# Closing a ReLU-and-mean kernel with one VectorE instruction over the last piece and the sums of the others

## The chip, the cores and the metric

The kernel runs on one core of one Trainium2 chip. The metric is the time of one execution on the device in microseconds, as the median of several runs. The engines that matter are DVE (VectorE), ACT (ScalarE), POOL (GpSimd), and SP (SyncE), which issues the transfers.

## The reference

```python
def reference(x):                       # x: float32, 32 x 512 x 1024
    relu_x = np.maximum(x, 0)
    return np.mean(relu_x, axis=-1).astype(np.float32)
```

There are 16384 rows of 1024 values, 67.11 MB in all; each row gives one number.

## The kernel before

Each of the 128 partitions holds 128 rows. Tiles of 16 rows are loaded through three buffers. ACT takes the even rows and DVE the odd rows; either makes ReLU and row sum in one instruction with an accumulator, whose read is a separate entry in the trace (0.08 us on DVE, 0.19 us on ACT). The last tile is loaded in ever smaller transfers, and its last row in three pieces of 512, 256 and 256 columns, so that little is left to do when the last bytes land. The end of the kernel is what the change is about:

```python
def act_row(nc, src, acc):
    nc.scalar.activation(out=src, in_=src, func=ACT.Relu, accum_out=acc)

def dve_row(nc, src, acc, init=None):
    nc.vector.tensor_scalar(out=src, in0=src, scalar1=0.0, scalar2=init,
                            op0=ALU.max, op1=ALU.add, accum_out=acc)
# ... loads and sums of all rows but the last two of each partition ...
    act_row(nc, prev[:, :512], part[:, 0:1])          # second-to-last row
    dve_row(nc, prev[:, 512:], part[:, 1:2])
    nc.gpsimd.tensor_scalar(out=res[:, J-2:J-1], ...)  # (a + b) * inv
    act_row(nc, last[:, :256], part[:, 2:3])          # piece 1, both engines
    dve_row(nc, last[:, 256:512], part[:, 3:4])
    nc.gpsimd.tensor_scalar(out=part[:, 4:5], ...)     # ACT's sum * inv
    act_row(nc, last[:, 512:640], part[:, 5:6])       # piece 2, both engines
    dve_row(nc, last[:, 640:768], part[:, 6:7], init=part[:, 3:4])
    nc.scalar.activation(out=part[:, 7:8], ...)        # ACT's two sums, scaled
    dve_row(nc, last[:, 768:], part[:, 8:9], init=part[:, 6:7])   # piece 3
    nc.vector.scalar_tensor_tensor(                    # closing: one column
        out=res[:, J-1:J], in0=part[:, 8:9], scalar=inv, in1=part[:, 7:8],
        op0=ALU.mult, op1=ALU.add)
    nc.sync.dma_start(out=outr, in_=res)
```

Of the kernel before, what the change touches and what calls it, by code (L numbers as in the profile page):

```python
# [1 line left out]

# [4 lines left out]

F32 = mybir.dt.float32
ALU = mybir.AluOpType
ACT = mybir.ActivationFunctionType  # L10
# [9 lines that stand above are left out]
    nc.vector.tensor_scalar(  # L20
        out=src, in0=src, scalar1=0.0, scalar2=init,
        op0=ALU.max, op1=ALU.add, accum_out=acc,
    )


def issue_ahead_of_entry_barrier(nc):


    entry, body = nc.cur_f.blocks[0].instructions, None
    for block in nc.cur_f.blocks[1:]:  # L30
        for k, ins in enumerate(block.instructions):
            if ins.opcode == "DMACopy":
                body, load = block.instructions, k
                break
        if body is not None:
            break
    first = body[load]
    assert first.engine == mybir.EngineType.SP and not first.sync_info.on_wait
    assert all(i.opcode == "DMACopy" or i.engine != first.engine for i in body[:load])
    del body[load]  # L40
    at = next(k for k, i in enumerate(entry) if i.engine == first.engine and i.opcode == "Drain")
    entry.insert(at, first)


@with_exitstack
def kernel(
    ctx: ExitStack,
    tc: tile.TileContext,
    x: bass.AP,
    out: bass.AP,  # L50
):
    nc = tc.nc
    P = nc.NUM_PARTITIONS
    xf = x.flatten_outer_dims()
    R, D = xf.shape
    assert R % P == 0
    J = R // P
    inv = 1.0 / D
    xr = xf.rearrange("(p j) d -> p j d", p=P, j=J)
    outr = out.flatten().rearrange("(p j) -> p j", p=P, j=J)  # L60
    xlast = xr[:, J - 1, :]

    NB = 16
    full = J // NB - 1

    row_pieces = [8, 4, 2, 1]
    assert sum(row_pieces) == NB - 1
    col_pieces = [512, 256, 256]
    assert sum(col_pieces) == D

    pools = ctx.enter_context(ExitStack())
    in_pool = pools.enter_context(tc.tile_pool(name="in", bufs=3))
    res_pool = pools.enter_context(tc.tile_pool(name="res", bufs=1))
    sums = res_pool.tile([P, J], F32)
    res = res_pool.tile([P, J], F32)
    part = res_pool.tile([P, 10], F32)

    def rows(xt, lo, n, j0):

        for k in range(lo, lo + n):  # L80
            j = j0 + k
            (dve_row if j % 2 else act_row)(nc, xt[:, k, :], sums[:, j:j + 1])

    def finish(lo, hi):
        nc.gpsimd.tensor_scalar(  # L85
            out=res[:, lo:hi], in0=sums[:, lo:hi], scalar1=inv, scalar2=0.0, op0=ALU.mult, op1=ALU.add,
        )

    for t in range(full):
        j0 = t * NB  # L90
        xt = in_pool.tile([P, NB, D], F32, name="xt")
        nc.sync.dma_start(out=xt, in_=xr[:, j0:j0 + NB, :])  # L92
        rows(xt, 0, NB, j0)

    j0 = full * NB
    xt = in_pool.tile([P, NB, D], F32, name="xt")
    prev, last = xt[:, NB - 2, :], xt[:, NB - 1, :]
    lo = 0
    for n in row_pieces:
        nc.sync.dma_start(out=xt[:, lo:lo + n, :], in_=xr[:, j0 + lo:j0 + lo + n, :])  # L100
        lo += n
    c = 0
    for w in col_pieces:
        nc.sync.dma_start(out=last[:, c:c + w], in_=xlast[:, c:c + w])
        c += w

    finish(0, j0)
    lo = 0
    for n in row_pieces[:-1]:
        rows(xt, lo, n, j0)  # L110
        lo += n
    finish(j0, j0 + lo)



    act_row(nc, prev[:, :512], part[:, 0:1])
    dve_row(nc, prev[:, 512:], part[:, 1:2])
    nc.gpsimd.tensor_scalar(  # L118
        out=res[:, J - 2:J - 1], in0=part[:, 0:1], scalar1=part[:, 1:2], scalar2=inv, op0=ALU.add, op1=ALU.mult,
    )  # L120
    act_row(nc, last[:, :256], part[:, 2:3])
    dve_row(nc, last[:, 256:512], part[:, 3:4])
    nc.gpsimd.tensor_scalar(  # L123
        out=part[:, 4:5], in0=part[:, 2:3], scalar1=inv, scalar2=0.0, op0=ALU.mult, op1=ALU.add,
    )
    act_row(nc, last[:, 512:640], part[:, 5:6])
    dve_row(nc, last[:, 640:768], part[:, 6:7], init=part[:, 3:4])
    nc.scalar.activation(  # L128
        out=part[:, 7:8], in_=part[:, 5:6], func=ACT.Identity, scale=inv, bias=part[:, 4:5],
    )  # L130
    dve_row(nc, last[:, 768:], part[:, 8:9], init=part[:, 6:7])
    nc.vector.scalar_tensor_tensor(  # L132
        out=res[:, J - 1:J], in0=part[:, 8:9], scalar=inv, in1=part[:, 7:8], op0=ALU.mult, op1=ALU.add,
    )
    nc.sync.dma_start(out=outr, in_=res)

    pools.close()
    tc.close()
    tc.compile()
    issue_ahead_of_entry_barrier(nc)  # L140


# [1 line left out]
_INS = ['x']  # L144
_OUTS = [((32, 512), 'float32')]


# [23 lines left out]
```

## Time and profile before

| | before |
|---|---|
| median time (3 runs) | 164.05 us (163.62 to 164.06) |
| profiled run: time, span | 163.88 us, 162.1 us |
| DVE, ACT, POOL busy | 46%, 43%, 1% |
| input transfer on the chain that ended last | 84% |

The chain that ended last is followed back from the last instruction. It says that the kernel is a long transfer with a short computation at its end. I use two marks throughout. **T0** is the start of the second-to-last row's first instruction (157.34 us before); what comes ahead of it is transfer. The **tail** runs from T0 to the end of the instruction that makes the last result (159.59), 2.25 us. The lines behind both are in the prediction below.

### The profile page before, as it was taken

The numbers are of one execution on the slowest core, as the hardware profiler recorded it, in microseconds if no ns is written. First come the engines' busy times: TensorE is split into PE (matmuls) and PEld (weight loads), VectorE is DVE, ScalarE is ACT, GpSimd is POOL, SyncE is SP. The second block draws the span as 40 slices with busy tenths as digits, with TensorE's granted clock in tenths as the row PEclk, the third lists the DMA queues.
The fourth block names the chain that finished last, engine by engine and source line by source line (L and its number), as shares of the span: only waits on it lengthen the run. The fifth ranks groups of instructions, "written<-read, shape, count | busy, mean of one in ns | idle before, by whom it ended". The sixth has DMA issues, their size and how long they took to land.

```text
span 162.1 us, 358 instructions
## 1 busy us (share of the span) xinstructions
DVE 74.7 (46%) x135; ACT 69.6 (43%) x134; POOL 1.2 (1%) x8
## 2 busy tenths in 40 slices
DVE  0000049700795009930199102990049800698993
ACT  3000049500793009910199002980049600696882
POOL 0000000000000000000000000000000000000001
DMA  8996996997997998998998999899898897998980
GB/s 275 501 485 291 518 501 291 501 501 323 469 518 340 437 518 356 420 518 356 420 520 374 404 501 404 388 501 404 388 518 388 388 518 332 437 445 384 420 311 17
DMA packets 2162, 67.19 MB, mean 415 GB/s; under 512 B 240, under 2 KB 624, under 8 KB 880
## 3 DMA queue, kind: packets, MB, share of 16 engines
q1 hardware_dynamic: 2160, 67.18, 96.6%
q14 instruction: 2, 0.02, 0.0%
HBM read 67.11 MB, written 0.07 MB: 414 GB/s over the span
## 4 chain that ended last, share of the span: by engine, by line
DMA 84%; DVE 13%; SPq 1%; issue 0%; DVEq 0%
DMA xt<-in_x_dram 84%; DVE xt L20 13%; SPq L100 1%; DVE res L132 0%; DVEq L20 0%; DVEq L132 0%; SPq L92 0%
## 5 line engine op out<-in xcount | busy, mean ns | idle before, releaser
L20 DVE TENSOR_SCALAR_CACHE_REDUCE xt<-xt 128x1024 f32<-128x1024 f32 (+1 forms) x65 | 73.7, 1195 | 84.7 <-DMA xt<-in_x_dram 84.3
L15 ACT ACTIVATE xt<-xt 128x1024 f32<-128x1024 f32 (+1 forms) x66 | 67.0, 1015 | 88.7 <-DMA xt<-in_x_dram 88.6
L15 ACT ACTIVATION_READ_ACCUMULATOR xt<-xt 128x1 f32 x66 | 12.3, 186 | 0.0
L20 DVE DVE_READ_ACCUMULATOR xt<-xt 128x1 f32 x65 | 5.4, 83 | 0.0
L85 POOL TENSOR_SCALAR res<-sums 128x112 f32<-128x112 f32 (+1 forms) x2 | 0.5, 252 | 156.7 <-DVE xt L20 156.7
L15 ACT ACT_TABLE_LOAD x1 | 1.3, 1283 | 0.8 <-PEq L155 0.8
L20 DVE TENSOR_SCALAR_CACHE_REDUCE xt<-xt,part 128x128 f32<-128x128 f32 (+1 forms) x2 | 0.8, 412 | 0.1
L128 ACT ACTIVATE part<-part 128x1 f32<-128x1 f32 x1 | 0.3, 294 | 0.1
L118 POOL TENSOR_SCALAR res<-part 128x1 f32<-128x1 f32 x1 | 0.3, 264 | 0.5 <-ACT xt L15 0.5
L132 DVE SCALAR_TENSOR_TENSOR res<-part 128x1 f32<-128x1 f32 x1 | 0.2, 159 | 0.1
L123 POOL TENSOR_SCALAR part<-part 128x1 f32<-128x1 f32 x1 | 0.2, 191 | 0.1
L20 DVE DVE_READ_ACCUMULATOR xt<-xt,part 128x1 f32 x2 | 0.2, 83 | 0.0
L155 POOL MEMSET const-bfloat16-1.0<- 128x1 bf16 x1 | 0.1, 101 | 0.0
L155 POOL MEMSET const-uint8-127<- 128x1 uint8 x1 | 0.1, 101 | 0.0
L155 POOL MEMSET const-float32-0.0<- 128x1 f32 x1 | 0.1, 98 | 0.2 <-issue 0.2
L155 POOL MEMSET const-float32-1.0<- 128x1 f32 x1 | 0.1, 98 | 0.0
## 6 DMA issues: line engine op xcount, KB each, us to landing
xt<-in_x_dram SPq DMA_DIRECT2D x1, 4096.0 KB, 39.0
xt<-in_x_dram SPq DMA_DIRECT2D x1, 2048.0 KB, 43.5
xt<-in_x_dram SPq DMA_DIRECT2D x1, 1024.0 KB, 45.5
xt<-in_x_dram SPq DMA_DIRECT2D x1, 512.0 KB, 46.4
xt<-in_x_dram SPq DMA_DIRECT2D x1, 256.0 KB, 46.5
xt<-in_x_dram SPq DMA_DIRECT2D x2, 128.0 KB, 42.7
xt<-in_x_dram SPq DMA_DIRECT2D x7, 49.1
out_dram<-res SPq DMA_DIRECT2D x1, 64.0 KB, 1.5
```

What stands on the lines that cost most here:

```text
L15: nc.scalar.activation(out=src, in_=src, func=ACT.Relu, accum_out=acc)
L20: nc.vector.tensor_scalar(out=src, in0=src, scalar1=0.0, scalar2=init, op0=ALU.max, op1=ALU.add, accum_out=acc,)
L85: nc.gpsimd.tensor_scalar(out=res[:, lo:hi], in0=sums[:, lo:hi], scalar1=inv, scalar2=0.0, op0=ALU.mult, op1=ALU.add,)
L100: nc.sync.dma_start(out=xt[:, lo:lo + n, :], in_=xr[:, j0 + lo:j0 + lo + n, :])
L118: nc.gpsimd.tensor_scalar(out=res[:, J - 2:J - 1], in0=part[:, 0:1], scalar1=part[:, 1:2], scalar2=inv, op0=ALU.add, op1=ALU.mult,)
L123: nc.gpsimd.tensor_scalar(out=part[:, 4:5], in0=part[:, 2:3], scalar1=inv, scalar2=0.0, op0=ALU.mult, op1=ALU.add,)
L128: nc.scalar.activation(out=part[:, 7:8], in_=part[:, 5:6], func=ACT.Identity, scale=inv, bias=part[:, 4:5],)
L132: nc.vector.scalar_tensor_tensor(out=res[:, J - 1:J], in0=part[:, 8:9], scalar=inv, in1=part[:, 7:8], op0=ALU.mult, op1=ALU.add,)
L155: nc = _bacc.Bacc("TRN2", target_bir_lowering=False, num_devices=1)
```

## The change

The last row gets a tile of its own, with two further columns. ACT takes the whole of piece 1 and DVE the whole of piece 2, and their sums go into these two columns, right behind piece 3. One scalar-tensor-tensor over the 258 columns then takes the maximum with 0 (which leaves the two sums as they are), multiplies by a tile filled with 1/1024, and accumulates: its accumulator is the mean. The intent is to get rid of the chain of small instructions that combines partial sums, above all of the last one.

```diff
-    part = res_pool.tile([P, 10], F32)
+    part = res_pool.tile([P, 2], F32)
+    last = res_pool.tile([P, D + 2], F32)
+    scale = res_pool.tile([P, D // 4 + 2], F32)
+    nc.gpsimd.memset(scale, inv)
...
-    act_row(nc, prev[:, :512], part[:, 0:1])
-    dve_row(nc, prev[:, 512:], part[:, 1:2])
+    act_row(nc, prev[:, :448], part[:, 0:1])
+    dve_row(nc, prev[:, 448:], part[:, 1:2])
...
-    (pieces 1 and 2 on both engines, the POOL and ACT scalings, piece 3)
+    act_row(nc, last[:, :512], last[:, D:D + 1])
+    dve_row(nc, last[:, 512:768], last[:, D + 1:D + 2])
     nc.vector.scalar_tensor_tensor(
-        out=res[:, J - 1:J], in0=part[:, 8:9], scalar=inv, in1=part[:, 7:8], op0=ALU.mult, op1=ALU.add,
+        out=last[:, 768:], in0=last[:, 768:], scalar=0.0, in1=scale, op0=ALU.max, op1=ALU.mult,
+        accum_out=res[:, J - 1:J],
     )
```

More of the change, by code (lines that the diff above doesn't have):

```diff
@@ L96 @@
     xt = in_pool.tile([P, NB, D], F32, name="xt")
-    prev, last = xt[:, NB - 2, :], xt[:, NB - 1, :]
+    prev = xt[:, NB - 2, :]
     lo = 0
@@ L120 @@
     )
-    act_row(nc, last[:, :256], part[:, 2:3])
-    dve_row(nc, last[:, 256:512], part[:, 3:4])
-    nc.gpsimd.tensor_scalar(
-        out=part[:, 4:5], in0=part[:, 2:3], scalar1=inv, scalar2=0.0, op0=ALU.mult, op1=ALU.add,
-    )
-    act_row(nc, last[:, 512:640], part[:, 5:6])
-    dve_row(nc, last[:, 640:768], part[:, 6:7], init=part[:, 3:4])
-    nc.scalar.activation(
-        out=part[:, 7:8], in_=part[:, 5:6], func=ACT.Identity, scale=inv, bias=part[:, 4:5],
-    )
-    dve_row(nc, last[:, 768:], part[:, 8:9], init=part[:, 6:7])
+    act_row(nc, last[:, :512], last[:, D:D + 1])
+    dve_row(nc, last[:, 512:768], last[:, D + 1:D + 2])
     nc.vector.scalar_tensor_tensor(
-        out=res[:, J - 1:J], in0=part[:, 8:9], scalar=inv, in1=part[:, 7:8], op0=ALU.mult, op1=ALU.add,
+        out=last[:, 768:], in0=last[:, 768:], scalar=0.0, in1=scale, op0=ALU.max, op1=ALU.mult,
+        accum_out=res[:, J - 1:J],
     )
```

## The prediction

> **What bounds the kernel now.** I read the page's busy row and its chain first, to see which resource carries the span:
>
> ```profile
> DVE 74.7 (46%) x135; ACT 69.6 (43%) x134; POOL 1.2 (1%) x8
> ...
> DMA 84%; DVE 13%; SPq 1%; issue 0%; DVEq 0%
> ...
> HBM read 67.11 MB, written 0.07 MB: 414 GB/s over the span
> ```
>
> Neither compute engine is half busy, and 84% of the chain is input transfer; 67.11 MB must come in, and the change takes no byte away. Only what follows the last bytes can move. So I read next when the last pieces land. The views of DMA issues, asked for one narrow stretch at a time, give for the three pieces of the last row (512, 256 and 256 columns) the issue and the time to landing; the timeline of the queue gives the start of each issue.
>
> ```profile
> 111.44 0.44 SPq L104 DMA_DIRECT2D xt<-in_x_dram  x1
> ...
> xt<-in_x_dram SPq DMA_DIRECT2D x1, 256.0 KB, 46.5
> ...
> xt<-in_x_dram SPq DMA_DIRECT2D x1, 128.0 KB, 46.4
> ...
> 119.59 0.33 SPq L104 DMA_DIRECT2D xt<-in_x_dram  x1
> ...
> xt<-in_x_dram SPq DMA_DIRECT2D x1, 128.0 KB, 39.0
> ```
>
> Piece 1 lands at 111.44 + 46.5 = 157.94. Piece 2's issue follows at about 111.93 (two issues end at 112.37, each 0.44 long), so it lands at 158.33. Piece 3 lands at 119.59 + 39.0 = 158.59. These are good to about 0.05 us, since the landing times are rounded. The second-to-last row lands at 157.31, where the chain changes from transfer to DVE. Then the timeline of the tail, from which the chain's DVE steps can be read off:
>
> ```profile
> 157.34 0.69 DVE L20 TENSOR_SCALAR_CACHE_REDUCE xt<-xt 128x512 f32<-128x512 f32 x1
> ...
> 157.97 0.42 DVE L20 TENSOR_SCALAR_CACHE_REDUCE xt<-xt 128x256 f32<-128x256 f32 x1
> ...
> 158.44 0.35 DVE L20 TENSOR_SCALAR_CACHE_REDUCE xt<-xt,part 128x128 f32<-128x128 f32 x1
> ...
> 158.83 0.48 DVE L20 TENSOR_SCALAR_CACHE_REDUCE xt<-xt,part 128x256 f32<-128x256 f32 x1
> 158.87 0.29 ACT L128 ACTIVATE part<-part 128x1 f32<-128x1 f32 x1
> 159.23 0.08 DVE L20 DVE_READ_ACCUMULATOR xt<-xt,part 128x1 f32 x1
> 159.43 0.16 DVE L132 SCALAR_TENSOR_TENSOR res<-part 128x1 f32<-128x1 f32 x1
> 159.65 0.35 SPq L135 DMA_DIRECT2D out_dram<-res  x1
> ```
>
> (The reader's columns are start, length, engine, line, operation.) The reader is to see that the row's last value is ready at 159.43 + 0.16 = 159.59, one microsecond after the last piece landed, and that all of the change lies in the 2.2 us between 157.34 and there. 2.2 us is 1.4% of the span, so even a tail of no length at all would not be a change of 2%.
>
> [...] the issues last 0.33 to 0.44 us, the landings are 39 to 46.5 us away, so I go by landings. [...] 1215, 685 and 419 ns for 1024, 512 and 256 columns are 1.04 ns a column plus 0.15 us. [...] The trace of before has this operation only on one column (159 ns), which can't decide it.
>
> **The change part by part.**
>
> *Removed:* on ACT the 128-column piece and the one-column scaling (0.29 + 0.29), on POOL the scaling of a partial sum (0.19), on DVE the 128-column reduction (0.35 + 0.08) and the closing one-column operation. On the path to the end the last costs 0.16 us plus the 0.12 us between the accumulator read's end (159.31) and its start[...]: 0.28 us that really go. ACT's and POOL's removed work ended at 159.16, beside DVE's, so it is worth nothing of its own.
>
> *Moved:* the second-to-last row is split 448/576 in place of 512/512. ACT's part becomes 0.05 us shorter (0.83 ns a column from its 630 and 416 ns), DVE's 64 x 1.04 = 0.07 us longer. DVE is then free at 157.97 + 0.07 = 158.04, and next needs piece 2 (158.33); ACT is free at 157.92 and next needs piece 1 (157.94). Both wait for landings anyway: worth 0.
>
> *Piece 1* goes wholly to ACT. Start 157.97; the 512-column activation before took from 157.34 to the end of its accumulator read at 157.87 + 0.19 = 158.06, that is 0.72 us. So its sum is there at 158.69[...].
>
> *Piece 2* goes wholly to DVE: start 158.33 + 0.03 = 158.36; 256 columns with accumulator read took 157.97 to 158.40 = 0.43 us, so the sum is there at 158.79.
>
> *The closing instruction* waits for DVE's own sum, ACT's sum, piece 3 (158.59) and the fill of the scale tile (over since the start). In the built program these four are spread over two event waits ahead of it and one on it, with DVE's own sum first. The one-column operation of before, with one event wait, started 0.12 us after the sum it needed; with a further one I estimate 0.16 us: start 158.79 + 0.16 = 158.95. It then streams 258 columns. [...] it takes 0.15 + 258 x 1.04 = 0.42 us, of which, as with the 256-column reduction, 0.43 us pass until the accumulator has been read out: result at 159.38. That is 159.59 - 159.38 = 0.21 us earlier than before. From there on (output issue, 1.5 us to landing, end) nothing changes.
>
> *Added elsewhere:* a memset of 258 columns on POOL at the start, where the first transfer needs until 41 us: hidden. The last row's own tile has no former user, so its transfers need no buffer, but they stay behind the others on the same queue[...]. The landing times should not move. [...]
>
> **Rivals.** *First, half rate for the closing instruction.* [...] + 0.27 us, result at 159.65, and the change costs 0.06 us. I give it three chances in ten. *Second, ACT as the new bound:* with 512 columns on ACT its sum comes at 158.69, only 0.1 us ahead of DVE's. If piece 1 lands later by 0.2 us, ACT is last; the closing instruction would start near 159.1 and save only about 0.1 us. *Third, the landing of the last piece is the bound:* were piece 3 to land late by 0.4 us or more, both kernels wait for it; the old one then needs 0.48 + 0.28 us after it and the new one 0.45, so the change would save up to 0.3 us. *Fourth, all is covered by scatter:* the transfers make 157.3 of the 162.1 us, and the runs of before differ by 0.44 us among themselves, more than any of these effects.
>
> **Range and chances.** The runs of before are 163.62, 164.05 and 164.06, the profiled one 163.88: mean 163.90. The expected saving is 0.7 x 0.21 - 0.3 x 0.06 = 0.13, with a little for landings that are less tight than I read: 0.15 us. So 163.75 us. The range comes from the scatter of the transfers (0.2 us either way for a median) and 0.2 us of effect: 163.35 to 164.15. A change of over 2% is 3.3 us, more than the whole tail; a chance of one in a hundred for slower and less for faster covers an accident of the transfers.
>
> **What would show each step right or wrong.** In the profile after, the chain should again be input transfer to about 157.3 and then DVE. The closing scalar-tensor-tensor of 128x258 should last about 0.42 us (0.69 would be the half-rate rival), end with an accumulator read, and start about 0.16 us after DVE's 256-column sum. The 256-column reduction should start at piece 2's landing, 0.2 to 0.3 us after the 576-column one ended: idle time on DVE released by a transfer. ACT's 512-column activation should end its read before DVE's. From the second-to-last row's first instruction to the result should be 2.04 us in place of 2.25. I am wrong if the landings of the last row shift, if the chain runs over ACT, or if the time moves by more than half a microsecond either way: then it is the transfers, not the tail.

DVE starts piece 2 at 158.36, its sum is there 0.43 us later (158.79), the closing instruction starts 0.16 us after that and its result is read out 0.43 us on, at 159.38, which is 0.21 us earlier than the 159.59 of before. That the closing instruction runs at the 1.04 ns a column of the one-source reductions was the estimate. The operation that the trace of before has on one column only is the scalar-tensor-tensor, and what its 159 ns can't decide is whether it runs at that rate. The three chances in ten were an estimate too, and the rival's 0.27 us are another 258 x 1.04 ns.

## The result

The changed kernel takes 163.63 us (median of 4 runs, 163.53 to 163.92), against 164.01 us (163.62 to 164.06, 4 runs) for the kernel before in the same rounds. The ratio is 0.9985, with a 95% interval of 0.9965 to 1.0005. Ratios here are the mean time of one kernel's runs over that of the other's of the same rounds, so they are not quite the ratio of the medians. By the 2% measure this is the same time.

The chain of the changed kernel, by engine and then by line, is again input transfer with DVE at its end:

```profile
DMA 84%; DVE 12%; SPq 1%; issue 0%; DVEq 0%
DMA xt<-in_x_dram 56%; DMA last<-in_x_dram 29%; DVE xt L20 11%; SPq L105 1%; SPq L109 0%; DVE last L20 0%; DVE last L126 0%; DVEq L126 0%; DVEq L20 0%; SPq L97 0%; DVEq L134 0%
```

The last row's transfers are now named after their own tile. Their times to landing (DMA issues by line: size of one, time from issue to landing; in the second line the median of two) are what they were:

```profile
last<-in_x_dram SPq DMA_DIRECT2D x1, 256.0 KB, 46.5
last<-in_x_dram SPq DMA_DIRECT2D x2, 128.0 KB, 42.7
```

And this is the timeline of the tail (start, length, engine, line, operation; in brackets the idle time before and what ended it):

```profile
157.22 0.75 DVE L20 TENSOR_SCALAR_CACHE_REDUCE xt<-xt 128x576 f32<-128x576 f32 x1
...
157.88 0.63 ACT L15 ACTIVATE last<-last 128x512 f32<-128x512 f32 x1
...
158.22 0.42 DVE L20 TENSOR_SCALAR_CACHE_REDUCE last<-last 128x256 f32<-128x256 f32 x1 [0.23 <-DMA last<-in_x_dram]
158.42 0.19 ACT L15 ACTIVATION_READ_ACCUMULATOR last<-last 128x1 f32 x1
158.57 0.08 DVE L20 DVE_READ_ACCUMULATOR last<-last 128x1 f32 x1
158.86 0.43 DVE L126 SCALAR_TENSOR_TENSOR last<-last,scale 128x258 f32<-128x258 f32 x1 [0.21 <-DVE last L20]
159.21 0.09 DVE L126 DVE_READ_ACCUMULATOR last<-last,scale 128x1 f32 x1
159.36 0.35 SPq L130 DMA_DIRECT2D out_dram<-res  x1
```

The reader is to see three things. T0 is 157.22 and the result is there at 159.21 + 0.09 = 159.30, so the tail is 2.08 us, 0.17 us shorter than before. DVE waits 0.23 us for piece 2 to land, so dealing out the earlier work differently could not have helped much. And 0.21 us pass between DVE's own sum (158.57 + 0.08 = 158.65) and the closing instruction, in which no engine computes. Most of the experiments turn on that gap.

The medians differ by 0.38 us, the means of the same runs by 0.25 and the tails by only 0.17. In the profiled runs the rest is T0, which differs from run to run; the table after the experiments shows by how much.

### The profile page after: what moved, and what is told of

It reads as the page before. It is cut to its first block, busy times and chain, and to the rows that moved or that the text cites. A ratio compares the mean times of both kernels' runs of the same rounds, so it can differ in the third digit from the quotient of the medians.

```text
span 161.8 us, 351 instructions
## 1 busy us (share of the span) xinstructions
DVE 74.3 (46%) x132; ACT 69.2 (43%) x131; POOL 1.3 (1%) x8
## 4 chain that ended last, share of the span: by engine, by line
DMA 84%; DVE 12%; SPq 1%; issue 0%; DVEq 0%
DMA xt<-in_x_dram 56%; DMA last<-in_x_dram 29%; DVE xt L20 11%; SPq L105 1%; SPq L109 0%; DVE last L20 0%; DVE last L126 0%; DVEq L126 0%; DVEq L20 0%; SPq L97 0%; DVEq L134 0%
## 5 line engine op out<-in xcount | busy, mean ns | idle before, releaser
L20 DVE TENSOR_SCALAR_CACHE_REDUCE xt<-xt 128x1024 f32<-128x1024 f32 x64 | 73.4, 1208 | 84.5 <-DMA xt<-in_x_dram 84.2
L15 ACT ACTIVATE xt<-xt 128x1024 f32<-128x1024 f32 x64 | 66.2, 1036 | 88.6 <-DMA xt<-in_x_dram 88.4
L15 ACT ACTIVATE last<-last 128x512 f32<-128x512 f32 x1 | 0.6, 629 | 0.0
## 6 DMA issues: line engine op xcount, KB each, us to landing
xt<-in_x_dram SPq DMA_DIRECT2D x1, 512.0 KB, 46.4
last<-in_x_dram SPq DMA_DIRECT2D x1, 256.0 KB, 46.5
```

## The experiments

The first four share their runs of the kernel before (median 164.03 us), the next four likewise (163.84 us); the ninth ran alone (163.78 us). All gave the right result.

### e1: the changed kernel once more

No edit. Expected:

> The changed kernel once more. Tail = from the start of the second-to-last row's first instruction to the end of the last instruction that makes the result (2.25 us before, 2.08 after in the first profiles). My theory (the closing fold removes one small instruction[...]): the tail is again 2.05 to 2.12 us, and the time 0.1 to 0.4 us below before. Rival (the 0.4 us between the two medians is scatter of the input transfer): the tail repeats at 2.08 but the time's difference comes out near 0.17 us, and wherever it is larger the end of the input moved too.

Measured: 163.54 us, ratio 0.9978 (0.9961 to 0.9996). T0 is 157.13, and the closing read starts at 159.10 and lasts 0.08 us, so the tail is 2.05 us. The gap before the closing instruction is 0.21 us again (158.54 to 158.75). The lines behind this are:

```profile
157.13 0.75 DVE L20 TENSOR_SCALAR_CACHE_REDUCE xt<-xt 128x576 f32<-128x576 f32 x1
...
159.10 0.08 DVE L126 DVE_READ_ACCUMULATOR last<-last,scale 128x1 f32 x1
```

The tail repeats, at the lower edge of what was expected. The time's difference does not quite: by medians it is 0.49 us, more than the 0.1 to 0.4 expected (by means 0.32). As the rival says, the end of the input moved too: in the profiled runs the tail is 0.20 us shorter and T0 0.21 us earlier. Over all, 25 runs of the kernel before average 163.893 us and the 8 of the changed one 163.655. That is 0.24 us with a scatter of 0.2 us a run, so the change is a little faster, and most of the amount is the tail.

### e2: the new dealing without the fold

```diff
-    nc.vector.scalar_tensor_tensor(... 258 columns, accum_out=res[:, J - 1:J])
+    dve_row(nc, last[:, 768:D], part[:, 2:3], init=last[:, D + 1:D + 2])
+    nc.vector.tensor_scalar(
+        out=res[:, J - 1:J], in0=part[:, 2:3], scalar1=last[:, D:D + 1], scalar2=inv,
+        op0=ALU.add, op1=ALU.mult)
```

> Pieces dealt out as in the changed kernel (all of piece 1 on ACT, all of piece 2 on DVE, own tile), but closed as before: a reduction of piece 3 started from piece 2's sum, then a one-column instruction that adds ACT's sum and scales. My theory (dealing the pieces out anew is worth nothing by itself, the fold is all): piece 2's sum at 1.43 us into the tail, reduction of piece 3 from 1.47 to 1.95, closing start 0.12 us later, 0.16 us long: tail 2.23 us, as before (2.25). Rival (fewer instructions on ACT, DVE and POOL, or the own tile, are the gain): tail near 2.08.

Measured: 164.05 us, ratio 1.0003 (0.9987 to 1.0018). In its timeline the reduction of piece 3 is followed by the small closing instruction, as before:

```profile
159.04 0.48 DVE L20 TENSOR_SCALAR_CACHE_REDUCE last<-last 128x256 f32<-128x256 f32 x1
159.44 0.08 DVE L20 DVE_READ_ACCUMULATOR last<-last 128x1 f32 x1
159.64 0.21 DVE L127 TENSOR_SCALAR res<-part,last 128x1 f32<-128x1 f32 x1
```

With T0 at 157.58 the tail is 159.85 - 157.58 = 2.27 us. The closing instruction takes 0.21 us in place of 0.16; without that the tail would be 2.22. (The 0.16 us expected for it was a miss. A likely reason is the operand with one value per partition, here ACT's sum: the closing instruction of before has a constant there and took 0.16 us. A 256-column reduction took 0.48 us with such an operand, its start value, and 0.42 us without, in this run and in the kernel before. That is 0.05 to 0.06 us in both pairs, and in the second nothing else differs.) So fewer instructions, the own tile and the new dealing bring about 0.03 us together: DVE starts piece 3 at 1.46 us into the tail in place of 1.49 (158.83 - 157.34 before). The rival, that these are the gain, falls.

### e3: the fold with the old dealing

```diff
-    act_row(nc, prev[:, :448], ...); dve_row(nc, prev[:, 448:], ...)
-    act_row(nc, last[:, :512], last[:, D:D + 1])
-    dve_row(nc, last[:, 512:768], last[:, D + 1:D + 2])
+    act_row(nc, prev[:, :512], ...); dve_row(nc, prev[:, 512:], ...)
+    act_row(nc, last[:, :256], last[:, D:D + 1])
+    dve_row(nc, last[:, 256:512], part[:, 2:3])
+    act_row(nc, last[:, 512:640], last[:, D + 1:D + 2])
+    dve_row(nc, last[:, 640:768], last[:, D + 2:D + 3], init=part[:, 2:3])
```

The two tiles have one more column each, and the fold runs over 259 columns.

> Pieces dealt out as before (both engines on pieces 1 and 2, rows split 512/512), but closed by the one fold over piece 3 and three sum columns (259 columns). My theory: DVE's 128-column sum is there at 1.45 us into the tail, the fold starts 0.21 us later and takes 0.44: tail 2.10 us, nearly all of the gain. Rival (the new dealing is the gain): tail 2.2 us or more.

Measured: 163.64 us, ratio 0.9981 (0.9966 to 0.9996). T0 is 157.28:

```profile
158.66 0.08 DVE L20 DVE_READ_ACCUMULATOR last<-last,part 128x1 f32 x1
158.95 0.43 DVE L128 SCALAR_TENSOR_TENSOR last<-last,scale 128x259 f32<-128x259 f32 x1 [0.21 <-DVE last L20]
159.30 0.08 DVE L128 DVE_READ_ACCUMULATOR last<-last,scale 128x1 f32 x1
```

The tail is 159.38 - 157.28 = 2.10 us, as expected: the fold alone brings 0.15 of the 0.17 to 0.20 us.

### e4: the same waits in another order

The closing instruction waits for four things. In the built program one of these waits stays on the instruction; the other three become two event waits in DVE's queue ahead of it (the trace shows both, 0.02 and 0.05 us long, and one of 0.02 us in the kernel before, which waits for two things). In the changed kernel DVE's own sum comes first, then transfer and ACT, then POOL on the instruction. Here the list of waits of this instruction is reordered after it is built, so that DVE's own sum stands on the instruction. No wait is taken away.

```diff
+def order_waits_of_closing(nc, names=["DVE_", "Act", "DMAHW", "Pool"]):
+    for block in nc.cur_f.blocks:
+        for k, i in enumerate(block.instructions):
+            waits = i.sync_info.on_wait if i.sync_info else []
+            if i.engine == mybir.EngineType.DVE and len(waits) == 4:
+                ...   # sort the waits by names, put the instruction back
     issue_ahead_of_entry_barrier(nc)
+    order_waits_of_closing(nc)
```

> The changed kernel with the same four waits of the closing instruction in another order: the transfer, then POOL and ACT, are waited for ahead of it, and DVE's own sum on the instruction itself. My theory (each event wait that still stands between the last sum and the instruction costs 0.05 to 0.1 us: 0.21 us with two, 0.12 with one, 0.04 with none in the kernel before's reductions): start 0.04 to 0.12 us after DVE's own sum (ACT's sum, 0.04 us earlier than DVE's, may then be the last), tail 1.95 to 2.0 us. Rival (0.21 us[...], whatever the order): start 0.21 us after, tail 2.08.

Measured: 163.46 us, ratio 0.9968 (0.9952 to 0.9985), with T0 at 157.25:

```profile
158.43 0.19 ACT L15 ACTIVATION_READ_ACCUMULATOR last<-last 128x1 f32 x1
158.59 0.08 DVE L20 DVE_READ_ACCUMULATOR last<-last 128x1 f32 x1
158.75 0.43 DVE L140 SCALAR_TENSOR_TENSOR last<-last,scale 128x258 f32<-128x258 f32 x1
159.10 0.08 DVE L140 DVE_READ_ACCUMULATOR last<-last,scale 128x1 f32 x1
```

The gap is 158.75 - 158.67 = 0.08 us in place of 0.21, and the tail is 159.18 - 157.25 = 1.93 us, slightly better than the 1.95 to 2.0 expected. So the 0.21 us are not the instruction's own preparation: they became 0.08 when only the order of the waits was changed. The tail is 0.32 us shorter than before and 0.12 to 0.15 shorter than in the changed kernel. In the same rounds its runs average 163.47 us, and those of e1 163.63; these two sets of four overlap, so against the changed kernel it is the tail that shows the gain.

### e5: the old split of the second-to-last row

```diff
-    act_row(nc, prev[:, :448], ...); dve_row(nc, prev[:, 448:], ...)
+    act_row(nc, prev[:, :512], ...); dve_row(nc, prev[:, 512:], ...)
```

> The changed kernel with the second-to-last row split 512/512 again. My theory (the new split only moves work inside waits for landings): ACT may start piece 1 up to 0.05 us later, which its slack of 0.04 us ahead of DVE's sum nearly absorbs: tail 2.05 to 2.10 us, against 2.05 and 2.08 in the two profiles of the changed kernel. Rival (the split was needed so that ACT's 512 columns don't become the last sum): ACT's sum after DVE's, tail 2.12 or more.

Measured: 163.6 us, ratio 0.9981 (0.9966 to 0.9996). T0 is 157.50, the result at 159.56, the tail 2.06 us. The lines are:

```profile
157.50 0.69 DVE L20 TENSOR_SCALAR_CACHE_REDUCE xt<-xt 128x512 f32<-128x512 f32 x1
...
158.48 0.42 DVE L20 TENSOR_SCALAR_CACHE_REDUCE last<-last 128x256 f32<-128x256 f32 x1 [0.28 <-DMA last<-in_x_dram]
...
159.47 0.09 DVE L126 DVE_READ_ACCUMULATOR last<-last,scale 128x1 f32 x1
```

DVE waits 0.28 us for piece 2 in place of 0.23, and starts it at the same 0.98 us into the tail as in e1. No gain of the new split shows.

### e6: one wait less

```diff
-    nc.gpsimd.memset(scale, inv)
+    nc.vector.memset(scale, inv)
```

> The changed kernel with the scale tile filled by VectorE at the start, so that the closing instruction waits for three things and one event wait stands ahead of it (transfer and DVE's own sum), ACT's sum on the instruction. My theory (every event wait after the last sum costs about 0.09 us): start 0.12 us after DVE's sum in place of 0.21, tail 1.96 to 2.0 us, the fill hidden under the first transfer. Rival (number of waits doesn't matter): 0.21, tail 2.05 to 2.08.

Measured: 163.48 us, ratio 0.9977 (0.9958 to 0.9995), with T0 at 157.21:

```profile
158.54 0.08 DVE L20 DVE_READ_ACCUMULATOR last<-last 128x1 f32 x1
158.72 0.43 DVE L126 SCALAR_TENSOR_TENSOR last<-last,scale 128x258 f32<-128x258 f32 x1
```

The gap is 0.10 us and the tail 159.15 - 157.21 = 1.94 us, both 0.02 us better than expected. The fill itself lasts 0.27 us and starts at 0.91 us, long before DVE's first row at 22.29. In the changed kernel the fill is over at 1.09 us, more than 150 us before the closing instruction, and the gap is 0.21 us: the wait for it had cost about 0.1 us. In the built program of the changed kernel two event waits stand ahead of the closing instruction from DVE's sum on, in that of this run one.

### e7: the rate of the closing instruction

```diff
-    col_pieces = [512, 256, 256]
+    col_pieces = [256, 256, 512]
```

ACT takes the first 256 columns, DVE the second, and the closing instruction 514.

> The changed kernel with pieces of 256, 256 and 512 columns, so that the closing instruction runs over 514 columns. It measures the rate of a two-source float32 reduction. [...] 0.43 + 256 x 1.04 = 0.70 us. At half rate[...]: 0.43 + 256 x 2.08 = 0.96 us. The time itself should be 0.1 to 0.3 us above the changed kernel's.

Measured in one run: 164.02 us, state unknown. DVE's 576-column reduction lasts 0.75 us in it, as in the fast runs, so the duration below can be compared. The line is:

```profile
159.03 0.69 DVE L126 SCALAR_TENSOR_TENSOR last<-last,scale 128x514 f32<-128x514 f32 x1 [0.32 <-DMA last<-in_x_dram]
```

(0.69 - 0.43) / 256 columns is 1.02 ns a column, the same as the one-source reductions of before (1.04). The 0.70 us expected at 1.04 ns a column hold; the half-rate rival asked for 0.96 us and falls. DVE's own sum is ready 0.32 us before this instruction (158.71), which now waits for its own piece to land. That piece lands no later than in the changed kernel: 158.90 (issue 119.84 + 39.06), or 1.31 us into the tail, against 1.30 there. The tail is 159.73 - 157.59 = 2.14 us. The time is 0.4 us above the changed kernel's rather than the 0.1 to 0.3 expected, most of it T0.

### e8: the kernel before with its two closing waits exchanged

The same reordering as in e4, applied to the kernel before: ACT's value on the event wait, DVE's own sum on the closing instruction.

> The kernel before with the two waits of its closing one-column instruction exchanged: ACT's value on the event wait, DVE's own sum on the instruction. My theory (0.12 us there is 0.04 us plus one event wait): start 0.04 us after the sum, tail 2.17 us in place of 2.25: about half of what the fold brought, without the fold. Rival (a one-column pointer operand costs the 0.12 us whatever the order): tail 2.25.

Measured: 163.79 us, ratio 0.9989 (0.9974 to 1.0004), with T0 at 157.11:

```profile
159.01 0.08 DVE L20 DVE_READ_ACCUMULATOR xt<-xt,part 128x1 f32 x1
159.13 0.16 DVE L146 SCALAR_TENSOR_TENSOR res<-part 128x1 f32<-128x1 f32 x1
```

The gap is 0.04 us in place of 0.12, and the tail 159.29 - 157.11 = 2.18 us. So a gain of 0.07 us, against the 0.17 that the change brought, was to be had in the old kernel by the order of two waits. The time's interval holds 1, so only the trace shows it. With the own sum waited for last in both kernels, the change is worth more and not less: 2.18 us here against 1.93 in e4, 0.25 us.

### e9: what was left of the gap in e4

On top of e4, pieces of 448, 320 and 256 columns: 64 columns go from ACT to DVE.

```diff
-    col_pieces = [512, 256, 256]
+    col_pieces = [448, 320, 256]
```

> The kernel with DVE's own sum waited for on the instruction, and 64 columns moved from ACT's piece to DVE's (pieces of 448, 320 and 256). It asks what set the 0.08 us that were left between DVE's sum and the closing instruction. My theory (ACT's sum, seen through the event wait, was the last): ACT's sum comes 0.05 us earlier, DVE's 0.07 us later, so DVE's is the last and the closing instruction starts 0.04 us after it, as the one-source reductions do; tail 1.94 to 1.97 us, no better than 1.93. Rival (0.08 us is what the two-source instruction needs after its own engine's sum): 0.08, tail 1.99 to 2.01 us.

Measured: 163.51 us, ratio 0.9988 (0.9968 to 1.0007), with T0 at 157.15:

```profile
158.24 0.19 ACT L15 ACTIVATION_READ_ACCUMULATOR last<-last 128x1 f32 x1
158.56 0.08 DVE L20 DVE_READ_ACCUMULATOR last<-last 128x1 f32 x1
158.68 0.43 DVE L140 SCALAR_TENSOR_TENSOR last<-last,scale 128x258 f32<-128x258 f32 x1
```

With ACT's sum well ahead, the closing instruction starts 0.04 us after DVE's, as the theory said. But the theory's reason isn't shown: DVE's sum also came 0.07 us later against the landing of piece 3, so e9 can't tell ACT's sum from that landing. The trace of e4 speaks for the landing. These are its two event waits:

```profile
L140 DVEq EVENT_SEMAPHORE  x2: 21/36/50, 158.6 to 158.6; - x2
```

Piece 3 landed at 158.55 there (issue 119.50 and 39.05 us to landing; these times are read from the packed trace, which has more digits than the views). The first event wait, for this transfer, ended at 158.60. The second, for POOL and ACT, began at 158.64, when ACT's sum was there (158.62), and took the 0.05 us that it also takes in e9, where that sum had been there for 0.12 us. The closing instruction followed at 158.75, 0.20 us after the landing. So it was most likely piece 3, seen through two event waits, that came last in e4.

The accumulator read ends at 159.12, so the tail is 159.12 - 157.15 = 1.97 us: what the wait gives is taken back by DVE's longer piece. Moving 64 columns gains nothing; smaller shifts were not tried, and 0.04 us is near the 0.03 by which the two profiles of the changed kernel differ.

### All profiled runs side by side

| run | T0 | last DVE sum to closing instruction | tail | time of this run | time - T0 - tail |
|---|---|---|---|---|---|
| before | 157.34 | 0.12 | 2.25 | 163.88 | 4.29 |
| after | 157.22 | 0.21 | 2.08 | 163.58 | 4.28 |
| e1 again | 157.13 | 0.21 | 2.05 | 163.47 | 4.29 |
| e2 dealing only | 157.58 | 0.12 | 2.27 | 164.15 | 4.30 |
| e3 fold only | 157.28 | 0.21 | 2.10 | 163.67 | 4.29 |
| e4 own wait last | 157.25 | 0.08 | 1.93 | 163.47 | 4.29 |
| e5 old split | 157.50 | 0.21 | 2.06 | 163.84 | 4.28 |
| e6 one wait less | 157.21 | 0.10 | 1.94 | 163.44 | 4.29 |
| e7 long third piece | 157.59 | (transfer) | 2.14 | 164.02 | 4.29 |
| e8 before, waits exchanged | 157.11 | 0.04 | 2.18 | 163.57 | 4.28 |
| e9 shifted | 157.15 | 0.04 | 1.97 | 163.41 | 4.29 |

The last column is 4.29 us to within 0.01 in all runs: what follows the result (output transfer and the end of the program) does not change. So the time of a run is T0 plus the tail plus 4.29 us. T0 goes from 157.11 to 157.59 with no pattern by kernel (both variants of the kernel before have 157.11 and 157.34, the others spread around them). These 0.48 us are scatter of the input transfer, as far as one profile of each kernel can tell, and are larger than any effect of the change. The mean times of all runs are a check: against the kernel before in the same rounds they put the kernels in nearly the order of the tails (e4 0.48 us faster, e6 0.38, the other folds of the full comparisons 0.25 to 0.32, e8 0.15, e2 0.08 slower). They mostly differ by some 0.1 us more than the tails do, so a small effect on T0 is neither shown nor excluded. This is why the trace decides here and the medians only agree.

## Why the prediction was right

**What bounds the kernel**: right. The chain is 84% transfer as before, the times to landing are the same, and the effect that can be shown lies in the tail. One sign was put wrongly: the chain was to be transfer to about 157.3 and then DVE, but it is transfer until piece 2 lands at 158.20, since DVE now waits for that landing. The prediction's own term for piece 2 has this right.

**Removed: 0.28 us that really go** (0.16 for the closing instruction, 0.12 for its wait): right. e2, which brings this pair back (as 0.21 and 0.12), has a tail of 2.27 us. e8 shows that 0.08 of the 0.12 us was the order of the two waits: with it changed, 0.04 us were left. That ACT's and POOL's removed work is worth nothing of its own holds to 0.03 us by e2, which also has that work removed and yet gains no more.

**Moved: worth 0**: right. e5 takes the new split back and its tail is 2.06 us, as the two of the changed kernel are to 0.02 us.

**Piece 1 and piece 2**: ACT's sum was to be there 1.35 us into the tail and DVE's at 1.45. Measured in the changed kernel are 1.39 (158.61) and 1.43 (158.65), so ACT was 0.04 us ahead in place of 0.10, mostly because its piece started 0.03 us later. ACT did not become the bound in any profile here, so the second rival didn't come true, but it was close.

**The closing instruction's start** is the term of the sum that was mis-sized. The prediction put 0.16 us for two event waits and the trace has 0.21, which is 0.05 us too little. It took the 0.12 us of one event wait and guessed a cheaper second one. The chain of the changed kernel, in order of time, shows both (DVEq is DVE's queue, "issue" time in which nothing that the profile shows was waited for):

```profile
158.66 0.03 issue
158.69 0.02 DVEq L126
158.71 0.05 issue
158.76 0.05 DVEq L126
158.81 0.05 issue
158.86 0.43 DVE last L126
```

In this chain each event wait takes 0.02 to 0.05 us, and another 0.05 us passes from one entry of the queue to the next. With none between the sum and its user, the gap is 0.04 us (e8, e9), with one 0.10 to 0.12 (before, e2, e6), with two 0.21 (after, e1, e3, e5).

**Its duration** of 0.42 us at 1.04 ns a column: right, with 0.43 us measured and 1.02 ns a column by e7. The first rival, to which three chances in ten were given, is out.

**The sum**: 0.21 us predicted with full rate, 0.17 and 0.20 us measured in the tails. e3 shows how it comes about: the fold starts at 158.95 - 157.28 = 1.67 us into the tail where the reduction of piece 3 had started at 1.49, takes 0.43 us in place of 0.48 (both to the end of the accumulator read), and needs no closing pair: 0.28 + 0.05 - 0.18 = 0.15 us. The new dealing adds some 0.03.

**Added elsewhere**: right. POOL's fill runs from 0.78 us and is over at 1.09; the pieces land 46.5, 46.4 and 39.1 us after their issue (46.5, 46.4 and 39.0 before), so the new tile doesn't show in them. In both kernels the issue of piece 3 waits 7.2 us for an earlier transfer to land. Eight are in flight in the kernel before at that time: two whole tiles, four groups of rows and two pieces. Piece 3 goes out (at 119.59) as the first of them lands (issue 70.30, 49.3 us later). One reading is wrong without harm: the first transfer lands at 22.3 us, and the 41 us in the chain belong to a later one.

**The number**: the saving had been lowered from 0.21 to 0.15 us, by weighing in the half-rate rival and adding a little for landings that turned out as read. With 0.21 us the number would have been 163.69; the 163.75 is 0.12 us above the median. That the difference of the medians is 0.38 us and not 0.17 is the luck of which runs were drawn, which the fourth rival named as the scatter that covers the effect. Half of the range was made of that scatter, and no change at all would have fallen into it too, so the time says little about the mechanism; the tail does.

What stays open is why T0 varies by 0.5 us from run to run; no run here took that apart.

## What to carry to other kernels

When a kernel is bound by a transfer, write its time as the moment the last data is usable plus a tail, and read the tail from the trace: effects of 0.1 us are plain there and lost in the medians (T0 scattered by 0.48 us here). In the tail count instructions and also the waits between them: put the wait that ends last on the instruction itself and let waits that are long over stand ahead of it (the gap went from 0.21 to 0.08 us in e4), or remove them by doing the early work on the waiting engine (to 0.10 us in e6). A closing step that is a sum can ride in the last large instruction as further columns at about 1 ns a column (1.02 in e7), where an instruction of its own cost 0.16 us and a gap of 0.12 us in the kernel before.
